# Unused columns behind the constants and in front of x, so that the operands of matmuls begin at multiples of 64 bytes

## The chip, the cores and the metric

The kernel runs on one core of a Trainium2 chip. The metric is the device time of the program in microseconds (us). An execution under the profiler has a span (first to last instruction) and a time of its own, which is a little longer. TensorE's clock, as granted during the profiled execution, was 0.995 of full speed on average.

## The reference, cut to what matters

One layer on x of 256 tokens by 1,024 features, all in float32. Two mixers run side by side and are gated; a gated feed-forward part with a short convolution follows.

```
h = rmsnorm(x)
q, k, v, u_pool, gate_logits = split(h @ w_in)         # 3*512 + 512 + 2*1024 columns
attn = causal attention of 8 heads of 64, with q and k normed and rotated
pooled = (trailing means over 2, 4, 8, 16 tokens - u) @ w_pool, scaled
gates = sigmoid(gate_logits + b_gate)
x = x + (gates0 * (attn @ w_branch_attn) + gates1 * (pooled @ w_branch_pool)) @ w_out
up = conv3(rmsnorm(x) @ w_up)                          # 1024 -> 2 * 2816
gate, val = split(up)
return x + (silu(gate) * val) @ w_down                 # 2816 -> 1024
```

## The kernel before

Every large product is made of three matmuls in the number format fp32r. Each operand is split into a high part (ScalarE rounds it, `high`) and a low part (VectorE subtracts the high part from the source, `low`); then high times high, low times high and high times low are added up in one PSUM bank (`mm3`, lines 90 to 92; in `project`, line 276). GpSimd makes the low parts of the feed-forward activations (`finish`).

Weights come in chunks of 1 MB, 8,192 bytes in each of the 128 partitions. A chunk lands in one of four `raw` buffers, is split into one of four `whi` and one of four `wlo` buffers, and the list `order` sets the order of chunks. `ahead`, `next_high` and `next_low` place the splitting of later chunks between other work by hand. At the end of the function each engine's instructions are tied to the order in which they were written.

The stages, in order: q, k and v (`project`): the activations `xhi`, `xlo` are loaded as stationary operand (128 columns) and the weights stream as moving operand (512 columns). From then on it is the other way round: the weights are loaded, 128 columns at a time, and activations stream with 256 columns, one for each token. These stages are the pool part's u (`ps_u`), the gates (`ps_g`) with the attention of the four head pairs in between (plain fp32 matmuls and transposes), the branches (`ps_bp`, `ps_ba`), the output map (`ps_out`, with the residual sum, `hhi` and `hlo` made by VectorE and ScalarE behind each tile), then 22 rounds of the feed-forward part: two tiles of `ps_up`, and eight groups of `ps_d` for the round three earlier.

Where a tile begins in a partition follows from the order of the pools: the constants (`const`), `raw`, `whi`, `wlo`, the lasting activations (`act`: `xq`, `xhi`, `xlo`, `qkT`, `vn`, `poolh`, `pooll`, `ath`, `atl`) and then temporary tiles (`tmp`, later `ffn` with the tiles `ah` and `al`). Each tile takes its bytes rounded up to a multiple of 32. `xq` holds 8 columns for the norm's factors, then for each of 8 slices 256 columns of x and 512 of the weights of q: 6,152 columns or 24,608 bytes, which is 32 more than a multiple of 64. What lies behind it is therefore 32 bytes off such a multiple.

Of the kernel before, what the change touches and what calls it, by code (L numbers as in the profile page):

```python
# [8 lines left out]
F32 = mybir.dt.float32  # L9
# [5 lines left out]
P = 128  # L15
S = 256
NT = S // P
D = 1024
KD = D // P
H = 8  # L20
DH = 64
AW = H * DH
# [28 lines left out]
STAGGER = 1  # L51
AHEAD = 4
FFN_AHEAD = 6
XCUTS = (1, 2, 4, 6, 8)


@with_exitstack
def hybrid_layer_kernel(ctx: ExitStack, tc: tile.TileContext, xq_d, par_d, wkv_d, wpg_d,
                        wpool_d, wba_d, wbp_d, wout_d, wup_d, wdn_d, out_d):
    nc = tc.nc  # L60

    const = ctx.enter_context(tc.tile_pool(name="const", bufs=1))
# [3 lines left out]
    act = ctx.enter_context(tc.tile_pool(name="act", bufs=1))  # L66
# [92 lines left out]
    def ahead(upto=0):  # L159

        next_high()
        next_low()
        if at[1] - sum(p[0] < used[0] for p in pieces) < upto:
            next_high()
            next_low()
# [7 lines left out]


    ones = const.tile([P, P], F32, name="ones")
    nc.vector.memset(ones, 1.0)


    xq_all = act.tile([P, KD + KD * (S + AW)], F32, name="xq")
    gmix = xq_all[:, 0:KD]  # L180
    xq = xq_all[:, KD:].rearrange("p (k c) -> p k c", c=S + AW)
    xT = xq[:, :, 0:S]
# [6 lines left out]
    cut = 0  # L189
    for k in XCUTS:  # L190
        end = KD + k * (S + AW)
# [421 lines left out]
    def value_done(i, g, uc):  # L613
        taps(uc[0], KF + i, uc[1])
        nc.gpsimd.tensor_tensor(uc[1], g[1], uc[1], ALU.mult)  # L615
        acch[i] = tmp.tile([P, S], F32R, tag="ah", bufs=LAG + 2, name=f"ah{i}")
        accl[i] = tmp.tile([P, S], F32R, tag="al", bufs=LAG + 2, name=f"al{i}")
        high(acch[i], uc[1])
        return uc[1]
# [4 lines left out]
    def down(i, ms):  # L624
        if i % 2 == 0 and i // 2 not in wd:
            wd[i // 2] = chunk("dn")
        hi, lo = wd[i // 2]
        for m in ms:
            sl = slice((i % 2) * D + m * P, (i % 2) * D + (m + 1) * P)
            o = acc[m // 2][:, (m % 2) * S:(m % 2 + 1) * S]  # L630
            first = i == 0 and m % 2 == 0
            nc.tensor.matmul(o, hi[:, sl], acch[i], start=first, stop=False, skip_group_check=True)  # L632
            nc.tensor.matmul(o, hi[:, sl], accl[i], start=False, stop=False, skip_group_check=True)  # L633
            nc.tensor.matmul(o, lo[:, sl], acch[i], start=False, stop=i == KF - 1, skip_group_check=True)  # L634
        if i % 2 == 1 and len(ms) == KD:
            spent.add(next(c for c in his if his[c] is hi))
# [29 lines left out]
    for i in range(1, KF):  # L666
# [11 lines left out]
        if i >= LAG:  # L678
# [4 lines left out]
            down(i - LAG, range(KD))  # L683
            ahead(FFN_AHEAD)
        done = value_done(i, ug, uv)
# [85 lines left out]
```

## Time and profile before

| | |
|---|---|
| median of 3 runs | 357.05 us (356.94 to 358.64) |
| profiled execution, its own time | 356.89 us |
| its span | 355.1 us |
| TensorE busy (matmuls) | 344.3 us |
| VectorE, ScalarE, GpSimd busy | 255.3, 195.4, 101.7 us |
| data moved | 62.76 MB, mean 177 GB/s |

TensorE's matmuls are pipelined: each is shown from its start to a modelled end, so that neighbours overlap; the distance from one start to the next is what a matmul costs in a row of them. PE stands for the matmuls, PEld for the loads of stationary operands, which lie beside them. DVE is VectorE, ACT ScalarE, POOL GpSimd. In the groups a row gives line, engine, operation, output and inputs, shape and count, then the busy time in us, the mean of one in ns, and the engine's idle time just before.

### The profile page before, as it was taken

To read this page: it belongs to the slowest core of one execution; us is meant where nothing else is said; L and a number is where in the kernel's file an instruction comes from. 1 tells how busy PE (TensorE), PEld (TensorE's weight loads), DVE (VectorE), ACT (ScalarE), POOL (GpSimd) and SP (SyncE) were. 2 spreads that over 40 slices of the span, in tenths; PEclk is the share of its full clock that TensorE was granted. 3 is DMA by queue.
4 is the path that set the end of the run, shared out by engine and by line. 5 is a ranking of instruction groups with operands and counts; after the bars stand their busy time and mean duration, and the time that the engine had idled before them with its cause. 6 is when DMAs were issued, how large, how long until landed. Compare 5 with 4: busy or idle time off the path is not lost.

```text
span 355.1 us, 6775 instructions
## 1 busy us (share of the span) xinstructions
PE 344.3 (97%) x2760; PEld 334.5 (94%) x2760; DVE 255.3 (72%) x401; ACT 195.4 (55%) x311; POOL 101.7 (29%) x127
## 2 busy tenths in 40 slices
PE   8999895999999999999999999999999999999996
PEld 6887794999999999999999999999999999999996
DVE  4879727944677597499789986667777777777743
ACT  5955614636464984566467565555555555556420
POOL 1008999100000006379232222121212121212140
PEclk9999998999999999999999999999999999999999
DMA  7985623244263464075534764646455453642003
GB/s 281 420 341 178 252 90 119 49 173 170 116 236 120 173 258 163 6 293 194 221 117 140 278 236 180 220 145 231 134 222 185 172 228 128 238 132 107 2 0 118
DMA packets 10254, 62.76 MB, mean 177 GB/s; under 512 B 1136, under 2 KB 2288, under 8 KB 3312
## 3 DMA queue, kind: packets, MB, share of 16 engines
q1 hardware_dynamic: 10224, 62.34, 48.3%
q8 instruction: 21, 0.34, 0.4%
q14 instruction: 9, 0.07, 0.1%
HBM read 61.29 MB, written 1.05 MB: 176 GB/s over the span
## 4 chain that ended last, share of the span: by engine, by line
PE 75%; POOL 8%; DVE 8%; DMA 3%; ACT 2%; issue 2%; SPq 1%; POOLq 0%
PE ps_up L91 11%; PE ps_up L90 11%; PE ps_up L92 11%; PE ps_d L633 6%; PE ps_d L632 6%; PE ps_d L634 6%; PE ps_g L90 5%; PE ps_g L91 4%; PE ps_g L92 4%; DMA raw_k<-in_wkv 3%; DVE lo_up L82 2%; DVE hlo L84 2%; POOL rh_k L294 1%; POOL rh_q L294 1%; PE ps_bp L90 1%
## 5 line engine op out<-in xcount | busy, mean ns | idle before, releaser
L91 PE MATMUL ps_up<-hlo,hi_up 128*128 128x256 f32 x352 | 98.5, 280 | 0.2 <-DVE hlo L84 0.2
L90 PE MATMUL ps_up<-hhi,hi_up 128*128 128x256 f32 x352 | 98.7, 280 | 0.0
L92 PE MATMUL ps_up<-hhi,lo_up 128*128 128x256 f32 x352 | 98.4, 280 | 0.0
L91 PEld LDWEIGHTS ps_up<-hlo,hi_up 128*128 128x128 f32 x352 | 66.2, 188 | 0.4 <-DVE hlo L84 0.4
L90 PEld LDWEIGHTS ps_up<-hhi,hi_up 128*128 128x128 f32 x352 | 66.2, 188 | 0.0
L92 PEld LDWEIGHTS ps_up<-hhi,lo_up 128*128 128x128 f32 x352 | 66.2, 188 | 0.0
L82 DVE TENSOR_TENSOR lo_up<-raw_up,hi_up 128x1024 fp32r<-128x1024 f32 x44 | 55.9, 1274 | 6.1 <-ACT hi_up L78 6.1
L615 POOL TENSOR_TENSOR c_v<-c_g,c_v 128x256 f32<-128x256 f32 x22 | 16.3, 740 | 120.7 <-DVE c_v L598 120.7
L633 PE MATMUL ps_d<-al,hi_dn 128*128 128x256 f32 x176 | 49.2, 280 | 0.0
L634 PE MATMUL ps_d<-ah,lo_dn 128*128 128x256 f32 x176 | 49.2, 280 | 0.0
L632 PE MATMUL ps_d<-ah,hi_dn 128*128 128x256 f32 x176 | 49.2, 279 | 0.0
L78 ACT ACTIVATE hi_up<-raw_up 128x1024 fp32r<-128x1024 f32 x44 | 44.9, 1045 | 0.0
L90 PE MATMUL ps_g<-xhi,hi_g 128*128 128x256 f32 x128 | 37.5, 293 | 0.0
L91 PE MATMUL ps_g<-xlo,hi_g 128*128 128x256 f32 x128 | 36.3, 284 | 0.0
L92 PE MATMUL ps_g<-xhi,lo_g 128*128 128x256 f32 x128 | 36.3, 284 | 0.0
L78 ACT ACTIVATE ah<-c_v 128x256 fp32r<-128x256 f32 x22 | 9.2, 418 | 45.9 <-POOL c_v L615 45.9
L634 PEld LDWEIGHTS ps_d<-ah,lo_dn 128*128 128x128 f32 x176 | 33.1, 188 | 0.0
L632 PEld LDWEIGHTS ps_d<-ah,hi_dn 128*128 128x128 f32 x176 | 33.1, 188 | 0.0
L633 PEld LDWEIGHTS ps_d<-al,hi_dn 128*128 128x128 f32 x176 | 33.1, 188 | 0.0
L545 POOL TENSOR_TENSOR xq<-xq 128x256 f32<-128x256 f32 x8 | 7.0, 887 | 74.1 <-issue 70.1
L82 DVE TENSOR_TENSOR lo_dn<-raw_dn,hi_dn 128x1024 fp32r<-128x1024 f32 x22 | 27.8, 1265 | 0.4 <-ACT hi_dn L78 0.4
L603 DVE TENSOR_TENSOR u_v<-ps_up,R 128x256 f32<-128x256 f32 x22 | 9.3, 422 | 26.1 <-PE ps_up L92 26.1
(191 smaller groups left out, 843.7 us busy)
## 6 DMA issues: line engine op xcount, KB each, us to landing
raw_up<-in_wup SPq DMA_DIRECT2D x22, 1024.0 KB, 4.8
raw_dn<-in_wdn SPq DMA_DIRECT2D x11, 1024.0 KB, 4.8
raw_g<-in_wpg SPq DMA_DIRECT2D x8, 1024.0 KB, 4.8
raw_o<-in_wout SPq DMA_DIRECT2D x4, 1024.0 KB, 4.8
xq<-in_xq SPq DMA_DIRECT2D x3, 768.0 KB, 7.3
raw_v<-in_wkv SPq DMA_DIRECT2D x2, 1024.0 KB, 14.0
raw_p<-in_wpg SPq DMA_DIRECT2D x2, 1024.0 KB, 6.3
raw_bp<-in_wbp SPq DMA_DIRECT2D x2, 1024.0 KB, 5.5
```

Source lines behind the costliest of these rows:

```text
L78: nc.scalar.activation(hi, src, AF.Copy, scale=scale)
L82: nc.vector.tensor_tensor(lo, src, hi.bitcast(F32), ALU.subtract)
L84: nc.vector.scalar_tensor_tensor(lo, src, scale, hi.bitcast(F32), ALU.mult, ALU.subtract)
L90: nc.tensor.matmul(out, sh, mh, start=start, stop=False, **kw)
L91: nc.tensor.matmul(out, sh, ml, start=False, stop=False, **kw)
L92: nc.tensor.matmul(out, sl, mh, start=False, stop=stop, **kw)
L294: nc.gpsimd.tensor_tensor(rh, ss, mhalf[:, 0:H], ALU.pow)
L603: nc.vector.tensor_tensor(u, ps[:, 0:S], R2, ALU.mult)
L615: nc.gpsimd.tensor_tensor(uc[1], g[1], uc[1], ALU.mult)
L632: nc.tensor.matmul(o, hi[:, sl], acch[i], start=first, stop=False, skip_group_check=True)
L633: nc.tensor.matmul(o, hi[:, sl], accl[i], start=False, stop=False, skip_group_check=True)
L634: nc.tensor.matmul(o, lo[:, sl], acch[i], start=False, stop=i == KF - 1, skip_group_check=True)
```

## The change

A tile `home` of 16 columns (64 bytes) is put behind `ones` among the constants, and GpSimd clears its first column. The tile `xq` gets 24 unused columns (96 bytes) at its front, and the program goes on with the rest of the tile.

```
+LEAD = 24
+HOME = 16
...
     ones = const.tile([P, P], F32, name="ones")
+    home = const.tile([P, HOME], F32, name="home")
+    nc.gpsimd.memset(home[:, 0:1], 0.0)
     nc.vector.memset(ones, 1.0)
...
-    xq_all = act.tile([P, KD + KD * (S + AW)], F32, name="xq")
+    xq_all = act.tile([P, LEAD + KD + KD * (S + AW)], F32, name="xq")[:, LEAD:]
     gmix = xq_all[:, 0:KD]
     xq = xq_all[:, KD:].rearrange("p (k c) -> p k c", c=S + AW)
```

The starts in a partition, from the tile sizes, as bytes beyond a multiple of 128 (a 0 or 64 is a multiple of 64):

| tiles | before | after |
|---|---|---|
| `ones`, `diag` | 0, 0 | 0, 64 |
| `ident` (the identity for transposes) | 96 | 32 |
| `raw`, `whi`, `wlo` (all weights) | 64 | 0 |
| x and the weights of q in `xq` (first slice) | 96 | 0 |
| `xhi`, `xlo`, `qkT`, `vn`, `poolh`, `pooll`, `ath`, `atl`, `mh`, `ml`, `hhi`, `hlo` | 96 | 0 |
| `sm`, `pT`, `qg`, `ah`, `al` | 96 | 0 |
| `an` | 32 | 64 |

The rows of instructions are the same on every engine but GpSimd. There, at the program's start, where the constants are made (`ident` is the identity, `mhalf` a constant for powers, `mask` the causal mask, `rcnt` counts), stands before:

```order
L759 MEMSET const-uint8-127 128x1
L766 UNCONDITIONAL_BRANCH
masks.py:197 MEMSET ident 128x128
masks.py:199 ISA
masks.py:199 AFFINE_SELECT ident<-ident 128x128
L207 MEMSET mhalf 128x8
```

and after:

```order
L763 MEMSET const-uint8-127 128x1
L770 UNCONDITIONAL_BRANCH
L179 MEMSET home 128x1
masks.py:197 MEMSET ident 128x128
masks.py:199 ISA
masks.py:199 AFFINE_SELECT ident<-ident 128x128
L211 MEMSET mhalf 128x8
```

One memset stands ahead of the identity, and nothing else has moved.

## The prediction

> **What bounds the kernel now.** I read the page's first block, then busy time by stretch, then the chain that ended last, then the matmuls' own starts in the timeline. First the page: TensorE is busy almost all of the span.
>
> ```profile
> span 355.1 us, 6775 instructions
> PE 344.3 (97%) x2760; PEld 334.5 (94%) x2760; DVE 255.3 (72%) x401; ACT 195.4 (55%) x311; POOL 101.7 (29%) x127
> ```
>
> By stretch (length; busy us and count of each engine; granted clock, DMA share, GB/s) the share is not the same everywhere:
>
> ```profile
> 68.00:148.00 80.00, 80.00 (x690) 79.34 (x689) 51.56 (x92) 45.20 (x86) 6.97 (x8) 1.00 0.44 158
> 150.00:172.00 22.00, 21.84 (x187) 21.63 (x186) 21.82 (x26) 13.85 (x18) 17.24 (x14) 1.00 0.66 240
> 176.00:345.00 169.00, 169.00 (x1451) 169.00 (x1450) 126.27 (x189) 96.83 (x146) 39.21 (x44) 1.00 0.46 163
> ```
>
> From 68 to 148 and from 176 to 345 us TensorE never pauses and the other engines have room; from 150 to 172 VectorE is full too (21.82 of 22). The chain (start, length, what) says who sets the end elsewhere:
>
> ```profile
> 4.84 11.99 DMA raw_k<-in_wkv
> ...
> 58.40 0.98 ACT qkT L313 x2
> 59.42 0.73 PE ps_s L425 x4
> ...
> 169.70 2.89 DVE lo_up L82 x2
> ...
> 351.86 0.42 DVE xq L696
> ```
>
> Up to 59.42 the chain starts with a load of k and ends with ScalarE's copy of the turned k, not with TensorE; there the matmuls of q, k, v and u lie beside it. TensorE sets the pace from 59.42 to 148, and from about 176 to 351.86: 8.6 + 80 + 169 + 6.9 = 264 us. Only there does a shorter matmul shorten the program.
>
> **The change: operand starts.** The tile sizes, placed one behind the other, give today's starts in a partition. Every high and low weight part begins at a multiple of 64 bytes; xhi, xlo and each activation operand behind them begin 32 bytes off one. In q, k and v the weights stream as moving operand, with 512 columns, and the activations are loaded; in all other fp32r matmuls the activations stream, with 256 columns, and the weights are loaded. So before's trace holds both cases side by side: moving aligned with stationary off (q, k, v), and moving off with stationary aligned (the rest). The printed lengths can't be used, since ends are modelled; starts can. Starts of 40 matmuls with the aligned moving operand, two to a row:
>
> ```profile
> 30.12 0.63 PE L276 MATMUL ps_v<-hi_v,xlo 128*128 128x512 f32 x2
> ...
> 39.45 0.63 PE L276 MATMUL ps_v<-hi_v,xhi 128*128 128x512 f32 x2
> ```
>
> (39.45 − 30.12) / 40 = 233.25 ns for 512 columns. Starts of 195 matmuls with the moving operand 32 bytes off:
>
> ```profile
> 250.86 0.28 PE L90 MATMUL ps_up<-hhi,hi_up 128*128 128x256 f32 x1
> ...
> 273.61 0.28 PE L632 MATMUL ps_d<-ah,hi_dn 128*128 128x256 f32 x1
> ```
>
> (273.61 − 250.86) / 195 = 116.67 ns for 256 columns. Twice 116.67 is 233.3: the time goes by columns, 0.456 ns each, and what a matmul pays once, whatever its width, is 2 × 116.67 − 233.25 = 0.1 ns. A moving operand that begins inside a 64-byte block touches 17 blocks where 16 would do; if a block were paid whole, that is 116.67 × 16/256 = 7.3 ns once per matmul of 256 columns and nothing in q, k, v. The rows leave 0.1 ns for it. I take 0.
>
> The weight side is as plain. Loads of xlo (32 bytes off, first row) and of hi_up (aligned, second row) show one mean:
>
> ```profile
> L276 PEld LDWEIGHTS ps_q<-hi_q,xlo 128*128 128x128 f32 x16 | 3.0, 188 | 0.7
> L91 PEld LDWEIGHTS ps_up<-hlo,hi_up 128*128 128x128 f32 x352 | 66.2, 188 | 0.4 <-DVE hlo L84 0.4
> ```
>
> So 0 for loads too, and in q, k, v a gain would in any case lie beside the chain. The identity that transposes use stays 32 bytes off; its matmuls lose nothing by that and gain nothing.
>
> [...]
>
> **The change: other engines.** The same shift moves operands of ScalarE and VectorE. Rows of 512 elements from a source 32 bytes off (hi_q reads xq; vn) against aligned ones (raw_pool):
>
> ```profile
> L78 ACT ACTIVATE hi_q<-xq 128x512 fp32r<-128x512 f32 x8 | 4.9, 618 | 2.2 <-DMA xq<-in_xq 2.2
> L78 ACT ACTIVATE hi_pool<-raw_pool 128x512 fp32r<-128x512 f32 x1 | 0.6, 620 | 0.0
> L265 DVE TENSOR_TENSOR vn<-vn 128x512 f32<-128x512 f32 x1 | 0.7, 694 | 0.0
> L82 DVE TENSOR_TENSOR lo_pool<-raw_pool,hi_pool 128x512 fp32r<-128x512 f32 x1 | 0.7, 661 | 0.0
> ```
>
> 618 against 620 on ScalarE: nothing. 694 against 661 on VectorE: at most 5%, from one instruction each. Were all of it alignment, in every VectorE operation, the stretch that VectorE fills could give 5% of 21.82: 1.1 us, less than a run can tell. I take 0, since wider ones read alike, 1227 against 1221:
>
> ```profile
> L265 DVE TENSOR_TENSOR vn<-vn 128x1024 f32<-128x1024 f32 x1 | 1.2, 1227 | 2.3 <-ACT vn L259 2.3
> L82 DVE TENSOR_TENSOR lo_k<-raw_k,hi_k 128x1024 fp32r<-128x1024 f32 x4 | 4.7, 1221 | 0.0
> ```
>
> **The change: one memset and the loads.** GpSimd gets one memset of 128x1 ahead of the identity. Its neighbours at the start:
>
> ```profile
> 0.34 0.10 POOL L759 MEMSET const-uint8-127<- 128x1 uint8 x1
> ...
> 2.33 0.25 DVE L216 RECIPROCAL rcnt<-rcnt 128x16 f32<-128x16 f32 x1 [1.33 <-POOL rcnt L213]
> ...
> 4.42 0.35 DVE L219 TENSOR_SCALAR xhi<-xq 128x256 fp32r<-128x256 f32 x1 [1.84 <-DMA xq<-in_xq]
> ```
>
> Such a memset is 0.10 us. It delays identity, mask and rcnt by that; VectorE takes the reciprocal 0.10 later and then waits 1.74 instead of 1.84 us for x. The cover is the first load; without it the price is 0.10 us. The loads keep number, size and order; x's first piece now lands 32 bytes off, its later pieces aligned, the reverse of today: 0. No wait is added, and no instruction but the memset enters any queue.
>
> **The sum.** 0 on the path. The profiled run took 356.89 us, 1.8 beside its span, and the median of the three runs is 357.05; they are 0.16 apart, so I forecast the median, 357.0. A measurement here tells about 0.5% (1.8 us) from no change.
>
> **Rivals.** *Faster: coarser blocks.* Not one fp32r operand today begins at a multiple of 128 bytes (weights 64 off, activations 96 off); after the change all of them do. If every 128 bytes of a misaligned stream cost some extra, it would show as time per column, as the rows do, and would vanish. What it could give is bounded by two places where plain fp32 matmuls stand between pairs of k matmuls: four loads with one column each (L236), and two passes of 256 columns with both operands at multiples of 128 (L247):
>
> ```profile
> 22.68 0.50 PE L236 MATMUL ps_n<-ones,vn 128*128 128x1 f32 x4
> 23.04 0.71 PE L276 MATMUL ps_k<-hi_k,xhi 128*128 128x512 f32 x2
> 23.59 0.63 PE L276 MATMUL ps_k<-hi_k,xlo 128*128 128x512 f32 x2
> ...
> 27.32 0.59 PE L247 MATMUL ps_n<-diag,ones 128*128 128x256 f32 x2
> 27.56 0.82 PE L276 MATMUL ps_k<-hi_k,xhi 128*128 128x512 f32 x2
> 28.21 0.63 PE L276 MATMUL ps_k<-hi_k,xlo 128*128 128x512 f32 x2
> ```
>
> 28.21 − 27.32 less a pair's 0.467 is 0.423, or 212 ns a pass; if a fp32r column needs half of such a pass's, 256 take 106 (an estimate). 23.59 − 22.68 − 0.467 = 0.443, or 111 ns for one load with next to no columns, so loads would be the next bound at 111. Over 264 us the gain is 264 × (1 − 111/116.67) = 12.8 us, or with loads as quick as 106, 264 × (1 − 106/116.67) = 24.1. I take the first, because that row shows the bound: 344.2, with 333 as the far end. VectorE would follow: 126.27 in 169 × 0.951 = 161 us is 79%. Against it: 64 and 96 bytes off give the same time per column to 0.1%, loads differ in nothing, and no row shows a gain.
>
> [...]
>
> *Slower: loads collide with streams.* After the change the streaming operand and the next load begin at the same place of a 128-byte block, where today they begin 32 bytes apart. If a load beside a stream gets slower by over 116.67 − 111 = 5.7 ns, loads set the pace over those 264 us. The nearest row of a disturbed load:
>
> ```profile
> L91 PEld LDWEIGHTS ps_g<-xlo,hi_g 128*128 128x128 f32 x128 | 24.8, 193 | 0.0
> ```
>
> 5 ns over 188: just under that point. Twice it, 10 ns, gives 264 × 4.3/116.67 = 9.7 us, or 367. Against it: the present loads overlap a whole stream, so that blocks of every offset already meet.
>
> *The shift misses its aim.* If a matmul reads the same number of blocks whatever the start, nothing moves; that is the forecast's own case.
>
> **How the numbers follow.** No change 0.63 (its own range 356.0 to 358.6, the spread of runs shown); faster by coarser blocks 0.28, because the offsets that it needs do not occur in the trace; slower by collisions 0.09. The predicted time is that of the first. For 8 in 10 the range must take in most of the second: down to 340 it holds some two thirds of it (0.19) beside the first case (0.61), and 359.5 on top adds small losses. The chances of the three signs are those of the cases.
>
> **What would show it.** Right: starts of ps_up and ps_d still 116.67 ns apart, of ps_v 233.3, VectorE full from 150 to 172, the page's busy times the same. Faster: 111 or less between starts in the up loop, while the stretch from 150 to 172 keeps its length. Slower: starts over 117 apart with PEld longer than 188. Wrong altogether, if q, k, v and the up loop change by different amounts per column: then alignment of one operand alone is what counts.

## The result and the profile after

Slower: a median of 362.52 us (360.97 to 363.34, four executions) against 357.41 us of before; the ratio is 1.0131, with a 95% interval of 1.0101 to 1.016. Ratios here leave out executions over 1.5% above the fastest of the same kernel; where a kernel's executions split into two groups that far apart, all are told.

The page of the changed kernel: first block, then two of the costliest groups.

```profile
span 361.5 us, 6776 instructions
PE 351.0 (97%) x2760; PEld 341.2 (94%) x2760; DVE 254.5 (70%) x401; ACT 195.6 (54%) x311; POOL 103.2 (29%) x128
...
L93 PE MATMUL ps_up<-hlo,hi_up 128*128 128x256 f32 x352 | 100.3, 285 | 0.0
L93 PEld LDWEIGHTS ps_up<-hlo,hi_up 128*128 128x128 f32 x352 | 67.0, 190 | 0.0
```

TensorE is busy 6.7 us longer, about the 6.4 us that the span grew by, and VectorE and ScalarE as long as before. By stretch, with the same columns as in the prediction:

```profile
68.00:148.00 80.00, 80.00 (x680) 79.34 (x679) 51.56 (x91) 45.39 (x86) 6.98 (x8) 1.00 0.44 158
150.00:172.00 22.00, 22.00 (x187) 21.98 (x187) 21.42 (x26) 14.79 (x20) 18.45 (x15) 1.00 0.68 239
176.00:345.00 169.00, 169.00 (x1410) 169.00 (x1410) 124.43 (x187) 95.88 (x143) 38.21 (x42) 1.00 0.46 165
```

TensorE is as full as it was, at the same clock, and gets through fewer matmuls: 680 for 690, and 1410 for 1451. So each of them costs more. Their starts in the timeline, first and last of 95 in the branches and of 185 in the feed-forward part:

```profile
129.78 0.28 PE L92 MATMUL ps_bp<-poolh,hi_bp 128*128 128x256 f32 x1
...
140.93 0.28 PE L93 MATMUL ps_ba<-atl,hi_ba 128*128 128x256 f32 x1
...
250.83 0.29 PE L93 MATMUL ps_up<-hlo,hi_up 128*128 128x256 f32 x1
...
272.91 0.29 PE L94 MATMUL ps_up<-hhi,lo_up 128*128 128x256 f32 x1
```

11.15 / 94 = 118.6 ns, and 22.08 / 184 = 120.0 ns, where before showed 116.67. The pace changes from the one to the other at 172.8 us, behind a break in the stream. Over the stretches that TensorE sets (59.42 to 148 and 175.8 us of the feed-forward part in before's profile) this is 88.6 × 1.9/116.7 + 175.8 × 3.3/116.7 = 1.4 + 5.0 = 6.4 us: all of the difference between the two profiles. The profiled execution is the slowest of the four of the changed kernel; the medians differ by 5.1 us.

In q, k and v, with 512 columns, it went the other way (starts of 44 matmuls, two to a row, up to the last row):

```profile
30.21 0.62 PE L280 MATMUL ps_v<-hi_v,xlo 128*128 128x512 f32 x2
...
40.43 0.63 PE L280 MATMUL ps_v<-lo_v,xhi 128*128 128x512 f32 x2
```

10.22 / 44 = 232.3 ns, where before showed 233.25. So the same shift made the wide matmuls a little quicker and the narrow ones slower.

### The profile page after: what moved, and what is told of

Same layout as the page of the kernel before. It is cut to its first block, busy times and chain, and to the rows that moved or that the text cites. A ratio compares the mean times of both kernels' runs of the same rounds, so it can differ in the third digit from the quotient of the medians.

```text
span 361.5 us, 6776 instructions
## 1 busy us (share of the span) xinstructions
PE 351.0 (97%) x2760; PEld 341.2 (94%) x2760; DVE 254.5 (70%) x401; ACT 195.6 (54%) x311; POOL 103.2 (29%) x128
## 4 chain that ended last, share of the span: by engine, by line
PE 75%; POOL 8%; DVE 8%; DMA 3%; ACT 2%; issue 2%; SPq 1%; POOLq 0%
PE ps_up L93 11%; PE ps_up L92 11%; PE ps_up L94 11%; PE ps_d L638 6%; PE ps_d L637 6%; PE ps_d L636 6%; PE ps_g L92 5%; PE ps_g L93 4%; PE ps_g L94 4%; DMA raw_k<-in_wkv 3%; DVE lo_up L84 2%; DVE hlo L86 2%; POOL rh_k L298 1%; POOL rh_q L298 1%; PE ps_bp L92 1%
## 5 line engine op out<-in xcount | busy, mean ns | idle before, releaser
L92 PE MATMUL ps_up<-hhi,hi_up 128*128 128x256 f32 x352 | 100.5, 285 | 0.0
L93 PE MATMUL ps_up<-hlo,hi_up 128*128 128x256 f32 x352 | 100.3, 285 | 0.0
L94 PE MATMUL ps_up<-hhi,lo_up 128*128 128x256 f32 x352 | 100.2, 285 | 0.0
L93 PEld LDWEIGHTS ps_up<-hlo,hi_up 128*128 128x128 f32 x352 | 67.0, 190 | 0.0
L92 PEld LDWEIGHTS ps_up<-hhi,hi_up 128*128 128x128 f32 x352 | 67.0, 190 | 0.0
L94 PEld LDWEIGHTS ps_up<-hhi,lo_up 128*128 128x128 f32 x352 | 67.0, 190 | 0.0
L636 PE MATMUL ps_d<-ah,hi_dn 128*128 128x256 f32 x176 | 50.1, 285 | 0.0
L637 PE MATMUL ps_d<-al,hi_dn 128*128 128x256 f32 x176 | 50.1, 285 | 0.0
L638 PE MATMUL ps_d<-ah,lo_dn 128*128 128x256 f32 x176 | 50.1, 285 | 0.0
```

The lines of the kernel that those rows point to most:

```text
L92: nc.tensor.matmul(out, sh, mh, start=start, stop=False, **kw)
L93: nc.tensor.matmul(out, sh, ml, start=False, stop=False, **kw)
L94: nc.tensor.matmul(out, sl, mh, start=False, stop=stop, **kw)
```

## The experiments

Below, a start is given in bytes beyond a multiple of 512, and d is the start of the streaming operand less that of the loaded one. In the stages with 256 columns before has the loads at 448 and the streams at 480 (d = 32), the changed kernel 0 and 128 (d = 128). Measured paces are distances of starts in the timeline.

**The change in pieces, and a grid of starts.** `home_only` and `lead_only` each make one half of the change; `memset_only` adds the instruction and moves no start:

```
memset_only:   nc.gpsimd.memset(mhalf, -0.5)
             + nc.gpsimd.memset(mhalf, -0.5)
```

`starts_grid` is no layer. It runs, for each pair of starts and with a few plain fp32 matmuls ahead of each row,

```
for k in range(8):       # twice; mh, ml, sh, sl begin at multiples of 512
    s, m = slice(so // 4 + 256 * k, + 128), slice(mo // 4 + 256 * k, + 256)
    matmul(ps, sh[:, s], mh[:, m]); matmul(ps, sh[:, s], ml[:, m]); matmul(ps, sl[:, s], mh[:, m])
```

> The 64 bytes behind ones alone: weights begin at multiples of 128, activations 32 bytes beyond. A (load and stream 32 apart, as before): 116.7 ns between starts, 357.4 us. B (stream not at a multiple of 128): 357.4. C: anywhere between 357 and 363.

> The 96 bytes in front of x alone: weights and activations both begin 64 bytes beyond a multiple of 128. A (0 apart): slow, 361 to 363 us. B (stream not at a multiple of 128): 357.4. C: anywhere between 357 and 363.

> One more memset on GpSimd at the same place of the program (a constant cleared twice), all starts as before. A and B: 357.4 us and 116.7 ns. C, if a small shift in time is enough to change the pattern: anywhere between 357 and 363.

> Not the layer: only fp32r matmuls of 256 columns, 48 in a row for each of 24 pairs of starts (the loaded operand's start, the streaming operand's start, in bytes beyond a multiple of 512), three times over, with one to three plain fp32 matmuls of varying width between the rows; ScalarE, VectorE and GpSimd idle. Read: distance of starts. Theory A, collision: equal starts modulo 128 for load and stream are slow (118.6 to 120 ns), 32 apart quick (116.7). Theory B, absolute: a stream that begins at a multiple of 128 is slow wherever the load begins. Theory C, chance: starts don't matter, and the three rows of one pair differ among themselves by as much as pairs do (116.7, 118.6, 120).

`home_only` (loads 0, streams 32, d = 32) took 0.9975 of before (0.9949 to 1.0001); `memset_only` 1.001 (0.9986 to 1.0034); `lead_only` (448 and 64, d = 128) 1.0092 (1.0056 to 1.0128), with 118.7 ns behind 176 us in its profile. So the columns in front of x cost the time, and neither the 64 bytes behind the constants nor the memset. B had 357.4 us for `lead_only`, whose streams begin at no multiple of 128, so this alone speaks against it; A's times came out for all three. The grid asks the same without the layer. In its timeline, rows with the stream at 0 and the load first at 0, then at 64:

```profile
176.76 0.28 PE L51 MATMUL ps_sAmA<-big_mh,big_sl 128*128 128x256 f32 x1
...
182.15 0.28 PE L51 MATMUL ps_sAmA<-big_mh,big_sl 128*128 128x256 f32 x1
...
226.12 0.28 PE L51 MATMUL ps_sCmA<-big_mh,big_sl 128*128 128x256 f32 x1
...
230.88 0.28 PE L51 MATMUL ps_sCmA<-big_mh,big_sl 128*128 128x256 f32 x1
```

5.39 / 45 = 119.8 ns and 4.76 / 42 = 113.3 ns. The same stream, with its start unchanged, is slow or quick by where the load begins. B falls: the stream's own alignment isn't what counts. C falls as a general answer: the three rows of a pair agreed to 0.4 ns in 21 of 24 pairs (the other three show two paces each). A was right that the pair counts, but wrong on the period of 128. And since all other engines were idle here, none of their work is needed for it.

**The distance.** `grid_fine` takes all multiples of 32, `grid_steps` steps of 8 bytes, `grid_wide` 512 columns. Three layers set d with LEAD alone or with HOME:

```
lead104_home32:  HOME = 32, LEAD = 104     # loads 64, streams 0:    d = 448
lead104:         no home,   LEAD = 104     # loads 448, streams 384: d = 448
lead120:         no home,   LEAD = 120     # both 448:               d = 0
```

> Not the layer: the same rows of 48 matmuls, with the load at 0 or at 448 bytes beyond a multiple of 512 and the stream at all sixteen multiples of 32, three times over. Theory D, distance: the pace hangs on d, the stream's start less the load's, modulo 512, so the sixteen values for the load at 448 are those for the load at 0 turned by 448: 120 at d = 0, 116.7 or 117.8 at 32, 118.7 or 120 at 128, 113.4 at 448. Theory E, places: the pair counts and not the distance alone (load 96 with stream 32, d = 448 too, took 117.8), so the two lists differ.

> Not the layer: rows of 48 matmuls of 256 columns, load at 0, stream at 168 to 208 and 432 to 464 in steps of 8 bytes, eight times over. D: 113.3 ns around 192 and 448, going over into the values of 160 (117.4 or 118.7) and 224 (118.3); the eight rows of one distance show how often the 113.3 pattern is taken. Rival, blocks of 32 bytes: every start from 192 to 216 takes what 192 takes.

> Not the layer: rows of 48 matmuls of 512 columns, load at 0, stream at the sixteen multiples of 32, three times over. If the extra over 256 columns belongs to the load (one collision for each load of 128 columns), a matmul of 512 columns has the same extra in ns as one of 256 at the same distance, 0 to 7 ns over some 226.7 (twice 113.3). If it goes by columns, as the prediction took it, each distance takes twice its time for 256 columns: 240 at d = 0, 233.4 at 32, 226.7 at 192.

> The layer with HOME = 32 and LEAD = 104 columns: weights begin at 64 and activations at 0 beyond a multiple of 512 (d = 448), the pair that took 113.4 ns. D and E alike: 113.4 ns between starts in the gates and the feed-forward part, 264 x (1 - 113.4/116.7) = 7.5 us less than before, 350 us. Rival F, the layer has another limit: at this pace VectorE or the loads of weights set the end, and it stays over 354.

> The layer with LEAD = 104 columns and no tile behind ones: weights at 448, activations at 384 (d = 448 again, at other places; none of the activations at 0 beyond a multiple of 512). D: 113.4 ns and 350 us. E: may be 117.8 ns, 359 us.

> The layer with LEAD = 120 columns and no tile behind ones: weights and activations both at 448 beyond a multiple of 512 (d = 0), every operand of an fp32r matmul at a multiple of 64. D and E: 120 ns, 264 x (120/116.7 - 1) = 7.5 us more than before, 365 us. Alignment to 64 bytes by itself, were it what counts: as after, 361 to 363, or better.

The grids (ns from start to start; several values are different rows of one distance):

| d modulo 256 | 256 columns | 512 columns |
|---|---|---|
| 0 | 119.6 to 120.0 | 226.7 to 227.4 |
| 32 | 116.7 or 117.8 | 233.3 |
| 64 | 117.8 | 229 |
| 96 | 120.0 | 233.2 to 233.6 |
| 128 | 118.7 or 120.0 | 232.3 or 233.3 |
| 160 | 117.4 or 118.7 | 234.3 |
| 192 | 113.4 or 117.8 | 233.3 |
| 224 | 118.3 | 233.3 |

The two lists of `grid_fine`, with the load at 0 and at 448, are the same when turned by 448: D holds, E falls, and the period is 256 bytes. Around 192 and 448 nothing is gained between multiples of 32: 119.0 to 120.4 at 8, 16 and 24 bytes from them (one row of 118.9 aside), so a quick start is one exact multiple of 32, not a neighbourhood. Both expectations of `grid_steps` fall with that, and both of `grid_wide` with the last column: for 512 columns they gave 233 or 240 ns at d = 0 and 226.7 at 192, and it is 227 and 233.3. The layer agrees: `lead120`, with d = 0 in q, k and v too, runs those at 227 ns in its profile.

With d = 0 and every fp32r operand at a multiple of 64, `lead120` took 1.0176 of before (1.0134 to 1.0217). Its starts, 194 of them:

```profile
250.73 0.28 PE L91 MATMUL ps_up<-hhi,hi_up 128*128 128x256 f32 x1
...
273.89 0.28 PE L92 MATMUL ps_up<-hlo,hi_up 128*128 128x256 f32 x1
```

23.16 / 193 = 120.0 ns, as the grid has it. The expected 365 us came out at 364.73. The opposite, d = 448, split: `lead104` took 351.63, 351.20, 357.81 and 357.62 us, `lead104_home32` 3 times 350.9 to 352.4 and 9 times 357.0 to 358.8. The quick ones lie 0.9 to 2.4 us above the expected 350, and F falls for them; the others need the second pattern of the table.

**Two patterns.** A profile of `lead104_home32` that took 357.02 us shows both (starts of 140 matmuls, then the three around a break, then the last of 193 that begin at 192.80):

```profile
175.75 0.28 PE L94 MATMUL ps_up<-hhi,lo_up 128*128 128x256 f32 x1
...
191.50 0.28 PE L92 MATMUL ps_up<-hhi,hi_up 128*128 128x256 f32 x1
...
191.95 0.28 PE L93 MATMUL ps_up<-hlo,hi_up 128*128 128x256 f32 x1
192.10 0.39 PE L94 MATMUL ps_up<-hhi,lo_up 128*128 128x256 f32 x1
192.33 0.28 PE L92 MATMUL ps_up<-hhi,hi_up 128*128 128x256 f32 x1
...
192.80 0.28 PE L93 MATMUL ps_up<-hlo,hi_up 128*128 128x256 f32 x1
...
215.41 0.28 PE L637 MATMUL ps_d<-al,hi_dn 128*128 128x256 f32 x1
```

15.75 / 139 = 113.3 ns up to a break around the matmul with lo_up at 192.10, which begins 0.15 us behind its neighbour and 0.23 ahead of the next, and 22.61 / 192 = 117.8 ns behind it, up to the end of the stream. The places of the operands don't change, so the distance allows two patterns here, and the change from one to the other falls on a break. (Other distances have two as well. At d = 32 the profiles of `home_only` and `memset_only` run at 117.8 behind 176 us, where before's ran at 116.7; at d = 128 `lead_only` keeps 118.7 there, in an execution of 361.16 us, where the changed kernel takes 120.0 in one of 363.34.) The next five runs ask what tips it. `lead40` puts d at 192 (loads 448, streams 128); the others change one thing each:

```
lead40, lead40_again:  no home, LEAD = 40
lead40_home16:         HOME = 16 with its memset, LEAD = 40    # loads 0, streams 192
lead40_memset:         lead40 + nc.gpsimd.memset(mhalf, -0.5) once more
lead40_places:         lead40, ones = const.tile([P, P + 16], ...)[:, 0:P]   # loads 0, streams 192
```

> The layer with LEAD = 40 columns and no tile behind ones: weights at 448, activations at 128 beyond a multiple of 512, so d = 192, where eight of nine rows of the grids took 113.3 ns and one 117.8, while at d = 448 five of twelve took 117.8. Theory D with period 256 and patterns that are chosen at each break of the stream: 350 to 352 us in most executions, fewer near 358 than LEAD = 104 had. Rival: d = 192 and d = 448 are the same thing and the grids' difference is chance; then executions split between 351 and 358 as before.

> The changed layer with LEAD = 40 in place of 24, HOME = 16 as it is: weights at 0, activations at 192 beyond a multiple of 512, d = 192 at other places than LEAD = 40 alone. Theory D: 351 to 352.5 us again, and if d = 192 is what keeps the 113.3 pattern, in all executions. Rival: that all five executions of LEAD = 40 stayed at 351 was chance, and here they split between 351 and 358.

> LEAD = 40 alone, with one more memset on GpSimd (a constant cleared twice), at the places of LEAD = 40. If the additional instruction's shift in time decides which pattern a break leaves behind: mostly near 358, as with HOME = 16. If the places decide: 351 to 352.5 in all executions.

> The places of LEAD = 40 with HOME = 16, without the memset (the tile ones is 16 columns longer instead). If the additional instruction decides: 351 to 352.5 in all executions. If the places (weights at 0, activations at 192) decide: mostly near 358.

> LEAD = 40 alone once more, beside the other two. If its places or its timing hold the 113.3 pattern: all executions at 351 to 352.5 again. If five of five was chance: a split between 351 and 358.

`lead40` stayed quick in 5 of 5 (351.14 to 352.52 us, 0.983 of before, 0.9807 to 0.9853), but `lead40_again`, the same kernel, in 1 of 6 (352.22, the others 357.9 to 359.2). `lead40_home16` was quick in 2 of 12, `lead40_memset` in 4 of 6, `lead40_places` in 2 of 6. So neither the places nor the memset decide it alone, and the five of five did not come again. Whether it was chance is not shown: the five ran on one chip, and `lead40_again`, `lead40_memset` and `lead40_places` on another. Nor does d = 192 hold the quick pattern better than 448: `grid_steps` took it in six of eight rows at each (and the expectation's five of twelve at 448 is six of fifteen by the rows of the two grids). In the quick profile of `lead40`, the starts of 195 matmuls, and then two stretches:

```profile
250.81 0.28 PE L92 MATMUL ps_up<-hlo,hi_up 128*128 128x256 f32 x1
...
272.80 0.28 PE L91 MATMUL ps_up<-hhi,hi_up 128*128 128x256 f32 x1
```

```profile
150.00:172.00 22.00, 21.28 (x188) 21.09 (x187) 21.81 (x27) 13.31 (x18) 17.23 (x14) 1.00 0.70 242
176.00:345.00 169.00, 169.00 (x1493) 168.93 (x1492) 128.17 (x194) 96.17 (x145) 37.89 (x44) 1.00 0.47 165
```

21.99 / 194 = 113.35 ns, 1493 matmuls where before had 1451, and VectorE still far from full behind 176 us.

**A break of one's own.** Every profile at d = 192 or 448 runs at 113.4 ns from 123 to 166 us and at 117.8 from 80 to 85, each time behind a fixed pair of attention transposes, while two breaks come out either way: the one at 192 us, a wait alone, and the one at 174, a wait and two plain fp32 matmuls of the norm (`ps_n`). So a fixed row of plain fp32 matmuls was put behind those:

```
+            if i == LAG + 2:                       # round 5 of the feed-forward part
+                px = bank("ps_break")
+                for t in range(6):                 # 2 in lead40_break2
+                    nc.tensor.transpose(px[:, t % 4 * P:(t % 4 + 1) * P], ident, ident)
             down(i - LAG, range(KD))
```

> LEAD = 40 with two plain fp32 transposes of the identity into a spare bank, after the second tile of ps_up in round 5 of the feed-forward part (about 197 us); their result is not used. Theory: a break of the stream chooses the pattern and it holds up to the next; a break by waiting chooses by chance, a break by a fixed row of fp32 matmuls chooses alike each time (behind the last attention transposes at 123 us every profile at d = 192 or 448 shows 113.3, behind those at 79 us 117). So the executions no longer split: all near 352 if two transposes leave 113.3 behind, as the two at 123 us do, or all near 358. Rival, chance at any break: they split as before.

> The same with six transposes in place of two. Theory: again no split, on the same side or on the other (six transposes stand before the stretch at 79 us that runs at 117). Rival, chance at any break: a split.

With six transposes all six executions were quick: 351.76 to 355.0 us, 0.9842 of before (0.9812 to 0.9873); 355.0 is the profiled one, and its span of 351.1 us is like the others'. With two, 11 of 12 took 357.6 to 358.9 and one 353.58. In the profile of the one with six, the break turns the pattern (91 starts up to it, 197 behind):

```profile
194.76 0.28 PE L93 MATMUL ps_up<-hhi,lo_up 128*128 128x256 f32 x1
...
205.36 0.28 PE L93 MATMUL ps_up<-hhi,lo_up 128*128 128x256 f32 x1
205.48 0.82 PE L687 MATMUL ps_break<-ident 128*128 128x128 f32 x6
...
207.74 0.28 PE L635 MATMUL ps_d<-ah,lo_dn 128*128 128x256 f32 x1
...
229.96 0.28 PE L91 MATMUL ps_up<-hhi,hi_up 128*128 128x256 f32 x1
```

10.60 / 90 = 117.8 ns ahead, 22.22 / 196 = 113.4 behind. The hope that two would leave the quick pattern was wrong, and so was the count in the expectations: ahead of 79 us, too, stand two transposes and not six. With the count put right, the attention itself shows what the two versions show. The same profile, behind two transposes and then behind six:

```profile
79.45 0.38 PE L469 MATMUL ps_a<-ident,an 128*128 128x128 f32 x2
...
79.79 0.28 PE L92 MATMUL ps_g<-xlo,hi_g 128*128 128x256 f32 x1
...
85.21 0.29 PE L93 MATMUL ps_g<-xhi,lo_g 128*128 128x256 f32 x1
85.33 0.82 PE L446 MATMUL ps_p<-ident,sm 128*128 128x128 f32 x6
...
86.34 0.28 PE L91 MATMUL ps_g<-xhi,hi_g 128*128 128x256 f32 x1
...
88.61 0.28 PE L93 MATMUL ps_g<-xhi,lo_g 128*128 128x256 f32 x1
```

5.42 / 46 = 117.8 ns behind the two, 2.27 / 20 = 113.5 behind the six. In all nine profiles at d = 192 or 448 the paces are these two behind the pairs at about 80, 94 and 110 us and behind the sixes at about 86, 102 and 116 us. But the pair ahead of 123 us leaves the quick pattern each time, and the six ahead of 72 us leave either, so the number alone is not the rule. A fixed row of matmuls does set the pattern, nearly always alike at one place of the program (quick in 6 of 6 executions with six, slow in 11 of 12 with two); why two leave the one and six the other was not found out. `lead40` without a row was not run beside these two, so the times show six against two, and the profiles what a row does. Of the versions run, `lead40_break6` beats both kernels in every execution.

## Why the prediction was wrong

- **What bounds the kernel**: right. The 264 us that TensorE sets, times the change of pace, give the whole difference of the two profiles, as worked out above.
- **The operand starts, the step that failed**: "the time goes by columns, 0.456 ns each", from 233.25 ns for 512 columns and 116.67 for 256. Each number was right, and their ratio was a coincidence of two distances: the loads of q, k, v and their streams stand at d = 480, where the grid has 233.3, and the later stages at d = 32, where it has 116.7. At one and the same distance it fails: d = 0 takes 120 for 256 columns and 227 for 512. I asked of each operand alone whether it was aligned, and took the price of the shift as 0; it was +1.9 and +3.3 ns for each matmul of 256 columns (the two patterns of the new distance) and 1 ns less for one of 512. So the signs that the prediction named came true: starts over 117 apart with loads over 188, and different changes in q, k, v and the up loop. Only what it drew from the second, that the alignment of one operand counts, is not so: it is the distance of the two.
- **The loads**: "So 0 for loads too", from one mean of 188 ns. Behind the change the mean is 190, 2 ns more, beside matmuls that cost 3.3 more: the loads' mean length didn't show what the new distance cost the stream.
- **Other engines, the memset, the transposes' identity**: right, 0; `memset_only` ended at 1.001, VectorE filled the stretch from 150 to 172 us as before (21.42 of 22 us), and a row of six transposes of the attention took 572 to 574 ns from its first start to the next matmul's before, 571 to 573 behind the change.
- **The rivals**: coarser blocks fall, since `lead120` and the pair 0 and 0 of the grid, with streams at multiples of 64 and of 512, are among the slowest of all (120.0 and 119.8 ns). The collision rival, at 0.09, had the right place, the pair of starts, and the right sign; its condition was wrong (not equal places in 128 bytes: d = 96 is as slow as d = 0, 120.0 against 119.6 to 120.0 ns, with a period of 256), and so was its price, since it asked for loads longer by over 5.7 ns.
- **The range**: 340 to 359.5 was opened for a gain and left 2.5 us for a loss. The loss was 5.1. No run shows the 340 us: the quickest execution of any version of the layer took 350.92 us (`lead104_home32`), and the least pace of all starts tried was 113.3 ns, where the rival for a gain had put 111.

## What to carry to other kernels

Where TensorE streamed fp32r without a pause, the pace hung on where the loaded and the streaming operand began relative to each other (113.3 to 120.0 ns for 256 columns). Padding each to a round number cost time here, since it put d from 32 to 128 (1.0131 of before), and another pad saved some (`lead40_break6`, d = 192, 0.9842). Measure start-to-start distances over a grid of starts in a kernel of matmuls alone (one run of some 0.6 ms held 32 pairs three times), set the distance by a few unused columns, and then look at the pace behind each break of the stream. And when two rows of a trace agree in a ratio, look for a third that differs in one thing only before drawing a rule from them.

## What the runs showed that I had not expected

For fp32r in these runs, 256 columns took 113.3 ns at best, and at d = 192 and 448 not in all executions. The slower paces look like a repeating sum, an estimate from the paces of the timelines and grids above: 4 × 116.67, 3 × 117.78 and 2 × 120 ns are each that many times 113.33 and 13.3 ns more, and 5 × 118.67 has 26.7 more. The starts, which the traces hold in whole ns, do repeat in groups of that length: behind 250 us before's distances run 120, 113 or 114, 115 or 116, 117 or 118 and so again, and the changed kernel's 119, 121, while `lead40`'s stay at 113 or 114. But no single distance is 13.3 ns longer than the best; the loss is spread over the group, so a single stall on one matmul of the group isn't what the starts show. In the changed kernel's profile a pattern, once taken, held for as long as the stream had no break (1,410 matmuls from 176 to 345 us, each 119 to 121 ns behind the one before). What it is that repeats every 256 bytes is open, as is whether other number formats behave so: only fp32r was tried.
